# Two products for the centring, gate products ahead of LayerNorm's sums, and first weights held behind the squares, in a one-core RWKV-7 and Conformer step

## The chip, the core and the metric

The kernel runs on one core of a Trainium2 chip. A core has five engines that run side by side, each through its own list of instructions in a fixed order: TensorE (PE) multiplies matrices, VectorE (DVE) does elementwise work of one or two operands, ScalarE (ACT) does elementwise functions, GpSimd (POOL) and SyncE (SP) hardly compute here and SP issues DMAs. An engine goes on until an instruction needs something that another engine has not finished; then it and all that stands behind it in its list waits. The metric is the device time of one execution in microseconds (us), the median of several.

## The reference, cut to what matters

One layer takes 2048 new tokens of one sequence ("prompt") and one token for each of 8 running sequences ("samples"). The lines below are the core of the reference; the parts that the change touches are the norms `mu`/`var` over 64 channels of a head, the norm `cm`/`cv` over 512 channels, and the state `conv_new`.

```
h = rms_norm(x, norm_pre_g)
proj = h @ w_in                       # r, k, v, z_r, two LoRAs, conv GLU, z_c, two gates
...                                   # token shift, decay, in-context rate
y_w, wkv_new = wkv7_scan(...)         # delta rule, per head, 16 heads of 64
mu = mean(y_w, axis=-1); var = mean((y_w - mu)**2, axis=-1)      # per head
y_gn = (y_w - mu) * rsqrt(var + GN_EPS) * gn_g + gn_b
branch_r = ((y_gn + bonus) * silu(z_r)) @ w_branch_r
u = u_in[..., :D_CONV] * sigmoid(u_in[..., D_CONV:])
c = depthwise_conv(concat([conv_st, u]), conv_w) + conv_b        # 31 taps
cn = (c - cm) * rsqrt(cv + LN_EPS) * ln_c_g + ln_c_b             # over 512 channels
branch_c = (silu(cn) * silu(z_c)) @ w_branch_c
conv_new = buf[:, -(CONV_W - 1):]
out = (sigmoid(g_r) * branch_r + sigmoid(g_c) * branch_c) @ w_out
y = x + rms_norm(out, norm_post_g)
```

## The kernel before

**Tiling.** The prompt's 2048 tokens go through in four blocks of 512 (`BS`). Channels lie on the 128 partitions, tokens along the free axis, so a usual tile is 128 x 512 f32. Block 0 also carries 8 columns of the samples, so its input products are 128 x 264 (two halves of 256 + 8). In each block eight "units" (pairs of heads, `unit_a` and `unit_b`, j = 0 to 7) run the delta rule.

**Products.** Large matrix products are f32 products made of three passes over the high and the low parts of both operands. A value is split by `split` (L136): the high part is an ACT copy to a narrower type (fp32r), the low part is a DVE subtraction of the high part from the value. A product of two operands kept as full f32 is done by the PE in two records for each 512 columns instead of one. Weights come from DRAM to `wraw` over SP's queue, are split into `w` (`load_split`, L144) and stored once more ("kept") for later blocks.

**Centring of the group norm.** After a unit's recurrence its outputs lie in the one PSUM bank named `py`. ACT copies the bank to the tile `gt`, the PE multiplies `gt` by the matrix `cent` (the identity less 1/64 within each head) as one full f32 product into the next `py` (helper `stat`, L366), ACT squares that, `ones_b` sums it into `pc`, and the scaling follows. There are 32 units, so 32 such products. Tiles of one tag share a fixed number of buffers: `tmp` 4, `x` 2, `gt` 1, `xs` 1, `wraw` 3, `w` 5; PSUM banks: `pg` 3, `pa` 2, `pb`, `pc` and `py` one each.

**The order.** The code is written block by block, and a list scheduler orders each engine's instructions ahead of the run by priority; `behind(...)` and `issue_after` make an instruction come after a given one in that order. The tables `FILL0`, `FILL1`, `FILL2` say which pieces of other work (conv products `u`, gates by number, "n" for LayerNorm's mean, "z" and "Z" for the two halves of the z gate) are written behind which unit of a block, so that the PE has products to do while a unit's chain of small steps is running. `FILL0` belongs to block 0.

**LayerNorm of the conv branch.** `conv_norm` (L764) adds four tiles on DVE, averages over channels with a product by `avg_c`, and subtracts; `conv_scale` (L775) squares, averages again, and applies scale and sigmoid. `conv_gate` (L794) does the product of the z gate, its sigmoid, and the last multiplication; each z gate tile lies in `tmp`.

**The start.** `stage_first` (L391) loads x by eight transfers, squares the eight tiles on ACT, adds on DVE, averages by a product with `avg_c` (`py<-tmp,avg_c`), takes Ln and Exp on ACT, scales x and splits it into `ht`. `gemm_first` (L433) loads and splits the first weights and does the first 192 products.

**Samples.** Their work ("decode") is put between the prompt's work of blocks 1 and 2. Small copies (128 x 8) take the samples' columns out of PSUM in block 0 on DVE. One DRAM to DRAM copy moves the samples' conv state.

Of the kernel before, what the change touches and what calls it, by code (L numbers as in the profile page):

```python
# [25 lines left out]
def rwkv7_conformer_step(  # L26
# [8 lines left out]
    BS = 512  # L35
# [164 lines left out]
    cent = const.tile([128, 128], F32, name="cent")  # L200
# [3 lines left out]
    stt(cent, ones_b, -1.0 / 64, ident, ALU.mult, ALU.add)  # L204
# [96 lines left out]
    FILL0 = ("u1", "u2", "u3", "u5", "6n", "7", "0", "4zZ")  # L301
# [46 lines left out]
    def shift_(b, v, q, dst):  # L348
        mu = pv("mu", q)
        for ps, sl in v.parts:  # L350
            act(dst[:, sl], ps, AF.Identity, scale=omm[:, q:q + 1])
        before = None if b == 0 else carry[:, q:q + 1]
        for ps, sl in v.parts:
            n = sl.stop - sl.start
            d = dst[:, sl]
            stt(d[:, 1:n], ps[:, 0:n - 1], mu, d[:, 1:n], ALU.mult, ALU.add)
            if before is not None:
                stt(d[:, 0:1], before, mu, d[:, 0:1], ALU.mult, ALU.add)
            before = ps[:, n - 1:n]
# [30 lines left out]

    def stage_first():  # L391
# [41 lines left out]
    def gemm_first(ht, cols):  # L433
# [3 lines left out]
        for h in range(2):  # L437
            for c0 in cols:
                ws[c0, h] = new([128, 2, 4, 128], "w", F32R)
                load_split(ws[c0, h], win(c0)[h], ("in", c0 // 128, h))  # L440
# [219 lines left out]
    def unit_b(b, j, parts):  # L660
# [49 lines left out]

        ys = new([128, BS], "gt")
        cp(ys, yps)
        pcen = stat(pyt, cent, ys)
# [31 lines left out]
    def glu(b, ht, ct):  # L745
# [3 lines left out]
        with tc.high_priority(HPU):  # L749
# [14 lines left out]
    def conv_norm(b, cs):  # L764
# [5 lines left out]
        with tc.issue_after(done[0].ins):  # L770
# [4 lines left out]
    def conv_scale(b, cs):  # L775
# [7 lines left out]
        with tc.issue_after(done[0].ins):  # L783
# [3 lines left out]
        for ct in range(CT):  # L787
# [4 lines left out]
            mul(cs[ct], cs[ct], s1)  # L792

    def conv_gate(b, ht, cs, c0):  # L794
        vs = gemm([hspec(b, ht, N_SHIFT + 2 * DC + (c0 + i) * 128) for i in range(2)])
        s2s = []
        for i, z in enumerate(vs):
            ct = c0 + i
            s2 = new([128, BS], "tmp")
            s2s.append(s2)  # L800
            with tc.high_priority(HPZ):
                sigmoid_v(s2, z)
                for ps, sl in z.parts:
                    mul(s2[:, sl], s2[:, sl], ps)
                if b == 0:
                    vcp(sconv[:, 2 * CT + ct, :], z.s[0])
# [145 lines left out]
    def decode_conv():  # L952
# [13 lines left out]
        with later(5000):  # L966
            nc.scalar.dma_start(out=nconv_s[0, :, 0:NH - 1, :], in_=state_conv[0, :, 1:NH, :])
# [11 lines left out]
        vcp(un[0:NS], ps[0:NS])  # L979
# [34 lines left out]
    def gate(b, ht, i0):  # L1014
# [3 lines left out]
        with tc.high_priority(HPG):  # L1018
            for i, v in enumerate(vs):
                for ps, sl in v.parts:  # L1020
                    act(s[:, i, sl], ps, AF.Exp, scale=-1.0)
                if b == 0:
                    vcp(gate_s[:, i0 + i, :], v.s[0])
# [42 lines left out]
    def stage_out(b, mg):  # L1066
# [15 lines left out]
        def finish(i):  # L1082
# [14 lines left out]
            nc.scalar.dma_start(out=yout, in_=osb[i][0:n])  # L1097

        for h in range(2):
# [53 lines left out]
    def fill(b, ht, cs, what):  # L1153
# [3 lines left out]
        elif what == "n":  # L1157
            while taps:
                pull(1)
            conv_norm(b, cs)  # L1160
# [133 lines left out]
```

## Time and profile before

| | |
|---|---|
| median of 3 runs | 2791.29 us (2786.7 to 2793.33) |
| profiled execution, its own time | 2793.45 us |
| its span | 2791.7 us |
| PE busy | 2675.3 us (96%) |
| PE weight loads (PEld) busy | 2133.7 us (76%) |
| DVE busy | 1768.0 us (63%) |
| ACT busy | 1388.4 us (50%) |
| DMA, mean | 164 GB/s |

The span is the stretch from the first to the last event of the trace; the execution's own time holds 1.8 us more around it. Busy time is time in which an engine has an instruction in work; a wait is idle time that ended when another engine, or a DMA, signalled. A product of the PE overlaps the next one, so that the time of one product in a row of them is the distance of their starts, not the duration that stands beside one.

### The profile page before, as it was taken

How to read it: one execution, taken by the hardware profiler on the slowest of the kernel's cores; microseconds unless marked ns; L12 is line 12 of the kernel's file. 1: busy time of each engine (PE TensorE's matmuls, PEld its weight loads, DVE VectorE, ACT ScalarE, POOL GpSimd, SP SyncE). 2: the span in 40 equal slices, each digit the busy share in tenths (PEclk: the TensorE clock that was granted, in tenths of full speed). 3: DMA queues.
4: the chain of work that ended last, by engine and by line, in shares of the span. 5: the costliest groups of instructions: out<-in, count | busy, mean ns of one | idle time of the engine just before them, and what ended most of it. 6: DMA issues, size and time to landing. Idle time of an engine off the chain costs nothing.

```text
span 2791.7 us, 55435 instructions
## 1 busy us (share of the span) xinstructions
PE 2675.3 (96%) x22800; PEld 2133.7 (76%) x22800; DVE 1768.0 (63%) x3856; ACT 1388.4 (50%) x3039; POOL 16.2 (1%) x61
## 2 busy tenths in 40 slices
PE   6999999989999998999999999999999999999998
PEld 6888888878877776776887777677798777777787
DVE  5688887667876547556576646676376755664412
ACT  5666656672344555656113565755411356566511
POOL 0000000000000000000000000000000000000000
PEclk9999999999999899999999999999999999999999
DMA  6555654547974253344666324244466522332484
GB/s 215 184 166 179 196 179 167 188 136 257 312 248 135 86 146 114 109 147 130 212 235 214 129 94 156 100 134 150 154 215 215 193 95 100 96 114 92 132 280 166
DMA packets 149648, 458.50 MB, mean 164 GB/s; under 512 B 18897, under 2 KB 24258, under 8 KB 149387
## 3 DMA queue, kind: packets, MB, share of 16 engines
q1 hardware_dynamic: 143441, 433.36, 47.0%
q10 hardware_dynamic: 5954, 21.60, 1.9%
q8 instruction: 179, 2.93, 0.4%
q14 instruction: 74, 0.61, 0.1%
HBM read 346.21 MB, written 109.16 MB: 163 GB/s over the span
## 4 chain that ended last, share of the span: by engine, by line
PE 58%; DVE 20%; ACT 14%; DMA 4%; issue 2%; SPq 0%; POOL 0%; DVEq 0%; ACTq 0%; POOLq 0%
PE pg L112 41%; PE pa L112 7%; DVE gd L100 4%; PE pc L112 4%; PE py L112 4%; DVE zr L610 4%; PE pb L112 2%; ACT sc L94 2%; DVE et L106 2%; DVE raw L106 2%; DMA wraw<-in_w_in_dram 2%; ACT tmp L94 2%; ACT xv L94 2%; ACT zbuf L94 1%; ACT keep L94 1%
## 5 line engine op out<-in xcount | busy, mean ns | idle before, releaser
L112 PE MATMUL pg<-ht,w 128*128 128x512 f32 (+1 forms) x7200 | 1539.8, 365 | 18.2 <-DVE sconv L109 6.5
L112 PEld LDWEIGHTS pg<-ht,w 128*128 128x128 f32 x7200 | 1172.8, 190 | 264.6 <-issue 63.9
L106 DVE SCALAR_TENSOR_TENSOR et<-u,cw,et 128x512 f32<-128x512 f32 x480 | 359.5, 749 | 8.2
L94 ACT ACTIVATE raw<-pg,omm 128x512 f32<-128x512 f32 (+1 forms) x155 | 93.8, 605 | 194.0 <-PE pg L112 189.8
L94 ACT ACTIVATE tmp<-tmp 128x512 f32<-128x512 f32 (+1 forms) x305 | 185.5, 630 | 5.0 <-DVE tmp L106 2.5
L112 PE MATMUL pg<-orr,w 128*128 128x512 f32 (+2 forms) x960 | 184.7, 349 | 0.0
L112 PEld LDWEIGHTS pg<-orr,w 128*128 128x128 f32 x960 | 154.7, 188 | 25.0 <-DVE x L100 0.2
L94 ACT ACTIVATE w<-wraw 128x512 fp32r<-128x512 f32 x162 | 101.4, 629 | 119.5 <-PE pg L112 70.5
L106 DVE SCALAR_TENSOR_TENSOR raw<-pg,prm,raw 128x511 f32<-128x511 f32 (+1 forms) x185 | 103.8, 573 | 84.6 <-ACT raw L94 83.8
L100 DVE TENSOR_TENSOR gd<-zr,gp 128x144 f32<-128x144 f32 (+10 forms) x512 | 139.9, 273 | 15.2
L610 DVE TENSOR_REDUCE zr<-gd 128x16 f32<-128x32 f32 (+15 forms) x512 | 136.9, 267 | 13.9 <-DVE gd L100 0.2
L100 DVE TENSOR_TENSOR w<-wraw,w 128x512 fp32r<-128x512 f32 x162 | 110.6, 685 | 46.3 <-ACT w L94 45.2
L94 ACT ACTIVATE gd<-sc 32x128 f32<-32x128 f32 x256 | 78.6, 307 | 114.5 <-DVE sc L100 108.4
L528 DVE TENSOR_TENSOR_SCAN tmp<-scanm,tmp 128x512 f32<-128x512 bf16 x32 | 39.1, 1223 | 137.3 <-ACT tmp L94 137.3
L94 ACT ACTIVATE xs<-pc,dk 128x64 f32<-128x64 f32 x224 | 70.2, 313 | 106.5 <-PE pc L112 106.0
L100 DVE TENSOR_TENSOR x<-x,pg 128x512 f32<-128x512 f32 (+1 forms) x80 | 46.1, 578 | 101.5 <-PE pg L112 36.4
L112 PE MATMUL pa<-ar,bk 64*64 64x128 f32 x2048 | 101.3, 279 | 5.2 <-DVE bk L100 3.1
L112 PEld LDWEIGHTS pa<-ar,bk 64*64 64x64 f32 x2048 | 77.5, 132 | 37.1 <-DVE bk L100 15.1
L94 ACT ACTIVATE x<-pg 128x512 f32<-128x512 f32 (+1 forms) x80 | 40.9, 511 | 123.7 <-PE pg L112 119.9
L100 DVE TENSOR_TENSOR sc<-pa,maskw 128x512 f32<-128x512 f32 x128 | 82.5, 684 | 30.7 <-PE pa L112 30.3
L94 ACT ACTIVATE sc<-pa 64x256 f32<-64x256 f32 (+1 forms) x192 | 73.1, 381 | 47.0 <-PE pb L112 43.7
L100 DVE TENSOR_TENSOR keep<-pa,raw 128x512 f32<-128x512 f32 x32 | 22.1, 692 | 109.5 <-PE pa L112 109.5
(359 smaller groups left out, 3694.8 us busy)
## 6 DMA issues: line engine op xcount, KB each, us to landing
w<-kept_in SPq DMA_DIRECT2D x366, 512.0 KB, 3.4
kept_in<-w SPq DMA_DIRECT2D x122, 512.0 KB, 3.8
wraw<-in_w_in_dram SPq DMA_DIRECT2D x122, 256.0 KB, 3.2
w<-kept_br SPq DMA_DIRECT2D x48, 512.0 KB, 4.1
w<-kept_out SPq DMA_DIRECT2D x40, 512.0 KB, 4.5
gate<-x ACTq DMA_DIRECT2D x24, 512.0 KB, 4.7
x<-gate SPq DMA_DIRECT2D x48, 256.0 KB, 4.1
w<-kept_bc SPq DMA_DIRECT2D x24, 512.0 KB, 3.2
```

The lines of the kernel that those rows point to most:

```text
L94: return nc.scalar.activation(out=out, in_=in_, func=func, scale=scale, bias=bias, **kw)
L100: return nc.vector.tensor_tensor(out=out, in0=a, in1=b, op=op)
L106: return nc.vector.scalar_tensor_tensor(out=out, in0=a, scalar=s, in1=b, op0=op0, op1=op1)
L112: return nc.tensor.matmul(out=out, lhsT=lhsT, rhs=rhs, start=start, stop=stop, **kw)
L528: nc.vector.tensor_tensor_scan(out=sw, data0=scanm.rearrange("p c t -> p (c t)"), data1=sw, initial=0.0, op0=ALU.mult, op1=ALU.add)
L610: nc.vector.tensor_reduce(out=zl[:, 0:n, t:t + 2], in_=pr[:, 0:n, :, 0:w], axis=AX.X, op=ALU.add)
```

## The change

1. The centring. `cent` is kept as fp32r. The unit's outputs are split: high part by an ACT copy into `gt`, low part by a DVE subtraction into tag `xs`. Two products, `cent` by high and `cent` by low, go into the next `py` bank in place of one f32 product.
2. LayerNorm. In block 0 the table puts "z" behind unit 5, "Z" and gate 7 behind unit 6, gates 0 and 4 behind unit 7. The mean (`conv_norm`) is written behind the first half's z product, the scale (`conv_scale`) behind the second half's; the z tiles move from `tmp` to tag `x`, and the multiplication by them into `conv_scale`.
3. The start. The splits of the first weights come behind the last square (ACT) and the last addition (DVE).
4. The samples' small copies of block 0 go from DVE to ACT (94 of them).
5. The DRAM to DRAM copy of the conv state goes from the start to a place behind a copy of the decode work in block 1.
6. The last block's end: its square goes to a scratch tile, the multiplication by `gb` is done on DVE ahead of the scale, and one DVE instruction and one DMA stand for each half.

```
-    cent = const.tile([128, 128], F32, name="cent")
+    cent_r = const.tile([128, 128], F32R, name="cent")
...
-    FILL0 = ("u1", "u2", "u3", "u5", "6n", "7", "0", "4zZ")
+    FILL0 = ("u1", "u2", "u3", "u5", "6n", "z", "Z7", "04")
...
-                vcp(sraw[:, i, q, :], v.s[i])
+                cp(sraw[:, i, q, :], v.s[i])
...
-                tt(rb, rb, sq, ALU.add)
+                added = tt(rb, rb, sq, ALU.add)
+        first[:] = last.ins, added.ins
...
+        with behind(*first):
+            for h in range(2):
+                for c0 in cols:
+                    ws[c0, h] = new([128, 2, 4, 128], "w", F32R)
+                    load_split(ws[c0, h], win(c0)[h], ("in", c0 // 128, h))
...
+        yh = new([128, BS], "gt", F32R)
+        yl = new([128, BS], "xs", F32R)
+        split(yh, yl, yps)
+        pcen = pyt()
+        mm(pcen, cent_r, yh, stop=False)
+        mm(pcen, cent_r, yl, start=False)
         ys = new([128, BS], "gt")
-        cp(ys, yps)
-        pcen = stat(pyt, cent, ys)
         act(ys, pcen, AF.Square)
...
-                vcp(sconv[:, ct, :], va.s[0])
-                vcp(sconv[:, CT + ct, :], vb.s[0])
+                cp(sconv[:, ct, :], va.s[0])
+                cp(sconv[:, CT + ct, :], vb.s[0])
...
+            mul(cs[ct], cs[ct], zgate[ct // 2][:, ct % 2])
...
-        s2s = []
+        s2 = zgate[c0 // 2] = new([128, 2, BS], "x")
...
-        if c0 == 0:
-            conv_scale(b, cs)
-        for i, s2 in enumerate(s2s):
-            mul(cs[c0 + i], cs[c0 + i], s2)
+        (conv_scale if c0 else conv_norm)(cs)
...
-        with later(5000):
-            nc.scalar.dma_start(out=nconv_s[0, :, 0:NH - 1, :], in_=state_conv[0, :, 1:NH, :])
...
-        vcp(un[0:NS], ps[0:NS])
+        with behind(cp(un[0:NS], ps[0:NS]).ins):
+            nc.scalar.dma_start(out=nconv_s[0, :, 0:NH - 1, :], in_=state_conv[0, :, 1:NH, :])
...
-                    stt(osb[i][0:n, hs], pts[i][0:n] if h else osb[i][0:n, hs], rstd[0:n], gb[0:n, hs],
-                        ALU.mult, ALU.mult)
-                    tt(osb[i][0:n, hs], osb[i][0:n, hs], xrs[i][0:n, hs], ALU.add)
+                    stt(osb[i][0:n, hs], osb[i][0:n, hs], rstd[0:n], xrs[i][0:n, hs], ALU.mult, ALU.add)
+                    (nc.scalar, nc.sync)[h].dma_start(out=yout[:, hs], in_=osb[i][0:n, hs])
...
-                    act(half, pts[i][0:n], AF.Square, accum_out=sq[i][0:n, h:h + 1])
-                    if not (b == NB - 1 and h == 1):
+                    if b == NB - 1:
+                        junk = new([128, 512], "tmp")
+                        act(junk[0:n], pts[i][0:n], AF.Square, accum_out=sq[i][0:n, h:h + 1])
+                        mul(half, pts[i][0:n], gb[0:n, h * 512:h * 512 + 512])
```

Three places in the engines' order. First DVE at the start, before: `w_329` and `w_336` are the first two weights of the first product (the subtraction makes their low parts), `tmp_219` the sum of squares, `x_200` and `x_201` the first four tiles of x.

```order
L100 TENSOR_TENSOR w_329<-wraw_330,w_329 128x512
L100 TENSOR_TENSOR tmp_219<-tmp_219,tmp_233 128x512
L100 TENSOR_TENSOR tmp_219<-tmp_219,tmp_236 128x512
L100 TENSOR_TENSOR tmp_219<-tmp_219,tmp_239 128x512
L100 TENSOR_TENSOR w_336<-wraw_337,w_336 128x512
L100 TENSOR_TENSOR w_343<-wraw_344,w_343 128x512
```

And DVE at the start now, from the last addition's neighbour to the first weight's low part (the scalings and splits of x in between are cut).

```order
L100 TENSOR_TENSOR tmp_219<-tmp_219,tmp_239 128x512
L226 TENSOR_REDUCE par_c_119<-ident_79 128x2
L109 COPY cw_129<-pb_130 128x124
L106 SCALAR_TENSOR_TENSOR x_200<-x_200,prm_127,tmp_219 128x512
...
L106 SCALAR_TENSOR_TENSOR orr_203<-orr_203,prm_127,tmp_219 128x512
L100 TENSOR_TENSOR ht_280<-pa_252,ht_280 128x2x8
L100 TENSOR_TENSOR w_329<-wraw_330,w_329 128x512
L100 TENSOR_TENSOR ht_280<-orr_203,ht_280 128x256
```

The low part of `w_329` stood between two additions, ahead of every scaling of x; now it is the last but one of the list that scales and splits all eight tiles of x. On the PE, twelve products stand ahead of the first that reads it.

Second, the PE around the centring of a unit of block 1, before: `py` and `pc` are the banks of the unit, `pg<-ht,w` are products of the next gate or projection.

```order
L112 MATMUL py_11969<-aw_11903,xs_11926 64x64 x2
L112 MATMUL pg_12365<-ht_8009,w_12363 128x512
L112 MATMUL pg_12365<-ht_8010,w_12363 128x512 x3
L112 MATMUL py_12004<-gt_12002,cent_100 128x512
L112 MATMUL pg_12365<-ht_8011,w_12363 128x512 x3
```

And the same place now.

```order
L112 MATMUL py_12001<-aw_11935,xs_11958 64x64 x2
L112 MATMUL pg_12401<-ht_8040,w_12399 128x512 x2
L112 MATMUL pg_12401<-ht_8041,w_12399 128x512 x3
L112 MATMUL pg_12401<-ht_8042,w_12399 128x512 x3
L112 MATMUL py_12038<-gt_12034,cent_100 128x512
L112 MATMUL py_12038<-xs_12035,cent_100 128x512
L112 MATMUL pg_12440<-ht_8035,w_12436 128x512 x3
```

Between the unit's last output product and the centring stood four large products; now eight do, and the centring is two records of one product each.

Third, the PE at the samples' LoRA products in block 1 (`pb<-u,orr`, eight columns each, sixteen in all), before.

```order
L112 MATMUL pg_11170<-ht_8009,w_11168 128x512 x2
L112 MATMUL pb_10591<-u_10582,orr_10588 128x8
L112 MATMUL pg_11170<-ht_8009,w_11168 128x512
L112 MATMUL pb_10591<-u_10582,orr_10588 128x8
L112 MATMUL pg_11170<-ht_8010,w_11168 128x512
L112 MATMUL pb_10591<-u_10582,orr_10588 128x8
L112 MATMUL pg_11170<-ht_8010,w_11168 128x512
```

And now.

```order
L112 MATMUL pg_11237<-ht_8036,w_11233 128x512
L112 MATMUL pb_10625<-u_10616,orr_10622 128x8 x8
L112 MATMUL pg_11237<-ht_8036,w_11233 128x512
L112 MATMUL pg_11237<-ht_8037,w_11233 128x512 x3
L112 MATMUL pb_10634<-u_10616,orr_10622 128x8 x8
```

The small products alternated one by one with large ones; now they stand in two groups of eight.

## Rows read from the trace of the kernel before

**Rows 1.** The page's first part: engine, busy us, share of span, instructions.
```profile
PE   2675.3 (96%) x22800; PEld 2133.7 (76%) x22800; DVE 1768.0 (63%) x3856; ACT 1388.4 (50%) x3039; POOL 16.2 (1%) x61
```

**Rows 2.** Waits of PE by releaser: us in total, times, longest us.
```profile
PE pb L112 <- DVE gd L612: 20.2, 22, 2.2
PE py L112 <- DVE tmp L100: 15.0, 1, 15.0
PE pg L112 <- DVE tmp L100: 10.9, 2, 6.8
...
PE pg L112 <- DVE sconv L109: 6.5, 4, 1.9
```

**Rows 3.** Timeline of the start: start, us, engine, line, operation, [idle before].
```profile
11.26 1.32 ACT L94 ACTIVATE tmp<-orr 128x512 f32<-128x512 f32 x2
15.92 0.63 ACT L94 ACTIVATE w<-wraw 128x512 fp32r<-128x512 f32 x1 [3.35 <-DMA wraw<-in_w_in_dram]
...
17.20 2.28 DVE L100 TENSOR_TENSOR tmp<-tmp 128x512 f32<-128x512 f32 x3
...
19.62 2.05 PE L112 MATMUL py<-tmp,avg_c 128*128 128x512 f32 x2 [14.98 <-DVE tmp L100]
...
21.70 0.69 ACT L94 ACTIVATE tmp<-py,eps_rms 128x512 f32<-128x512 f32 x1 [0.16 <-PE py L112]
...
24.24 0.63 ACT L94 ACTIVATE tmp<-tmp 128x512 f32<-128x512 f32 x1 [0.23 <-DVE ht L100]
...
24.90 2.74 DVE L106 SCALAR_TENSOR_TENSOR x<-x,prm,tmp 128x512 f32<-128x512 f32 x4 [0.68 <-ACT tmp L94]
...
26.37 1.03 PE L112 MATMUL pg<-ht,w 128*128 128x264 f32 x3 [2.58 <-ACT ht L94]
```

**Rows 4.** Timeline of PE where the first 192 products end.
```profile
52.12 0.53 PE L112 MATMUL py<-ht,w 128*128 128x264 f32 x3
52.48 1.75 PE L112 MATMUL pg<-ht,w 128*128 128x264 f32 x13
```

**Rows 5.** Timeline of a unit's centring in block 1.
```profile
997.63 1.65 PE L112 MATMUL pg<-ht,w 128*128 128x512 f32 x6
...
997.99 0.61 ACT L94 ACTIVATE gt<-py 128x512 f32<-128x512 f32 x1
...
999.11 1.02 PE L112 MATMUL py<-gt,cent 128*128 128x512 f32 x2
...
1001.13 1.02 PE L112 MATMUL pc<-gt,ones_b 128*128 128x512 f32 x2
...
1001.99 1.02 PE L112 MATMUL pa<-tmp,ones_b 128*128 128x512 f32 x2
```

**Rows 6.** Timeline of PE, a run of large products in the last block.
```profile
2689.78 4.54 PE L112 MATMUL pg<-orr,w 128*128 128x512 f32 x19
2694.15 0.39 PE L112 MATMUL pg<-xv,w 128*128 128x512 f32 x1
```

**Rows 7.** Groups by form: DVE's low parts (count: ns min/median/max, first and last start).
```profile
L100 DVE TENSOR_TENSOR orr<-gt,orr x32: 675/684/694, 133.5 to 2642.1; 128x512 fp32r<-128x512 f32 x32
```

**Rows 8.** Timeline at a small copy in block 0.
```profile
152.57 0.16 DVE L109 COPY sconv<-pg 128x8 f32<-128x8 f32 x1
...
152.78 1.57 PE L112 MATMUL pg<-ht,w 128*128 128x264 f32 x10 [1.94 <-DVE sconv L109]
```

**Rows 9.** Windows: length, busy us of PE, PEld, DVE, ACT, POOL; PEclk; DMA.
```profile
612.00:628.00 16.00, 11.98 (x47) 9.67 (x48) 14.14 (x26) 11.36 (x21) 0.00 (x0) 0.79 0.29 83
...
1100.00:1112.00 12.00, 6.78 (x18) 4.78 (x19) 12.00 (x32) 5.88 (x10) 0.00 (x0) 0.72 0.19 79
948.00:970.00 22.00, 22.00 (x62) 14.50 (x62) 7.88 (x29) 2.87 (x11) 0.00 (x0) 0.61 0.17 55
```

**Rows 10.** Groups by form within 948 to 970 us: count, busy us, mean ns.
```profile
L112 PE MATMUL pb<-u,orr 64*128 64x8 f32 x32 | 8.2, 329 | 0.0
```

**Rows 11.** Timeline of the last DVE work before the last DMA.
```profile
2786.70 1.28 DVE L100 TENSOR_TENSOR orr<-orr,x 128x512 f32<-128x512 f32 x2
```

More of the change, by code (lines that the diff above doesn't have):

```diff
@@ L203, in rwkv7_conformer_step @@
         nc.gpsimd.memset(ones_b[s, s], 1.0)
-    stt(cent, ones_b, -1.0 / 64, ident, ALU.mult, ALU.add)
+    stt(cent_r, ones_b, -1.0 / 64, ident, ALU.mult, ALU.add)
+    cent = f32(cent_r)
     id2 = const.tile([128, C], F32, name="id2")
@@ L389, in stage_a @@
         return ht
+    first = []
     def stage_first():
@@ L436, in gemm_first @@
         views, ws = [], {}
[L437 to L440, printed above, removed]
+        with behind(*first):
[3 more added lines that the diff above has]
+                    load_split(ws[c0, h], win(c0)[h], ("in", c0 // 128, h))
         for i, _ in enumerate(cols):
@@ L762, in glu, with conv_norm @@
         return acc
-    def conv_norm(b, cs):
+    def conv_norm(cs):
         sm = new([128, BS], "tmp")
@@ L769, in conv_norm @@
             tt(sm, sm, cs[ct], ALU.add)
-        with tc.issue_after(done[0].ins):
+        with behind(done[0].ins):
             ps = stat(pgt, avg_c, sm)
@@ L773, in conv_norm, with conv_scale @@
             tt(cs[ct], cs[ct], ps, ALU.subtract)
-    def conv_scale(b, cs):
+    def conv_scale(cs):
         sm = new([128, BS], "tmp")
@@ L782, in conv_scale @@
             tt(sm, sm, sq, ALU.add)
-        with tc.issue_after(done[0].ins):
+        with behind(done[0].ins):
             ps = stat(pgt, avg_c, sm)
@@ L792, in conv_scale @@
             mul(cs[ct], cs[ct], s1)
+            mul(cs[ct], cs[ct], zgate[ct // 2][:, ct % 2])
+    zgate = [None, None]
     def conv_gate(b, ht, cs, c0):
         vs = gemm([hspec(b, ht, N_SHIFT + 2 * DC + (c0 + i) * 128) for i in range(2)])
-        s2s = []
+        s2 = zgate[c0 // 2] = new([128, 2, BS], "x")
         for i, z in enumerate(vs):
-            ct = c0 + i
-            s2 = new([128, BS], "tmp")
-            s2s.append(s2)
             with tc.high_priority(HPZ):
-                sigmoid_v(s2, z)
+                sigmoid_v(s2[:, i], z)
                 for ps, sl in z.parts:
-                    mul(s2[:, sl], s2[:, sl], ps)
+                    mul(s2[:, i, sl], s2[:, i, sl], ps)
                 if b == 0:
-                    vcp(sconv[:, 2 * CT + ct, :], z.s[0])
-        if c0 == 0:
-            conv_scale(b, cs)
-        for i, s2 in enumerate(s2s):
-            mul(cs[c0 + i], cs[c0 + i], s2)
+                    cp(sconv[:, 2 * CT + c0 + i, :], z.s[0])
+        (conv_scale if c0 else conv_norm)(cs)
     def conv_split(b, cs):
@@ L1022, in gate @@
                 if b == 0:
-                    vcp(gate_s[:, i0 + i, :], v.s[0])
+                    cp(gate_s[:, i0 + i, :], v.s[0])
         act(s, s, AF.Ln, bias=1.0)
@@ L1096, in finish @@
                 tt(osb[i][0:n], osb[i][0:n], xrs[i][0:n], ALU.add)
-            nc.scalar.dma_start(out=yout, in_=osb[i][0:n])
+                nc.scalar.dma_start(out=yout, in_=osb[i][0:n])
         for h in range(2):
@@ L1117, in sums @@
                     half = osb[i][0:n, h * 512:h * 512 + 512]
-                    act(half, pts[i][0:n], AF.Square, accum_out=sq[i][0:n, h:h + 1])
-                    if not (b == NB - 1 and h == 1):
+                    if b == NB - 1:
+                        junk = new([128, 512], "tmp")
+                        act(junk[0:n], pts[i][0:n], AF.Square, accum_out=sq[i][0:n, h:h + 1])
+                        mul(half, pts[i][0:n], gb[0:n, h * 512:h * 512 + 512])
+                    else:
+                        act(half, pts[i][0:n], AF.Square, accum_out=sq[i][0:n, h:h + 1])
                         cp(half, pts[i][0:n])
@@ L1159, in fill @@
                 pull(1)
-            conv_norm(b, cs)
         elif what in "zZ":
```

## The prediction

> **What bounds the kernel now.** I read the page's busy times first, then the waits of the PE, then the timeline at each of its longest waits, and the windows for the clock there. The PE is busy for 2675.3 us, 96% of a span of 2791.7 [rows 1]: it is the bound, and what it does not fill is 116 us. So the change can gain only where it takes PE work away, closes a wait of the PE, or lets the PE run at its full 2.4 GHz where it ran at 1.2; work moved between DVE (63%) and ACT (50%) counts only where the PE waits for it. The list of PE waits [rows 2] names the places: 15.0 us once at the start, 10.9 us in two waits for LayerNorm's sums (6.8 and so 4.1), 6.5 us in four waits for a small copy, and 20.2 us in 22 waits for small DVE steps of the units (`gd`), which no edit touches. The windows [rows 9] show the second cost: around the two LayerNorm waits the granted clock is 0.79 and 0.72, and around the samples' LoRA products, where the PE never idles, 0.61.
>
> All sums are made against the profiled execution's own 2793.45 us (its span and 1.8 us around it). The median shown is 2791.29, lower by 2.16, which I take off at the end.
>
> **The centring (32 units).** A full f32 product of 128 x 512 takes 1001.99 - 1001.13 = 0.86 us from start to start, in two records [rows 5]. A product of the new kind, with fp32r operands, is like those of the large run, 19 in 2694.15 - 2689.78 = 4.37 us, 0.23 each [rows 6]. One f32 product goes, two of the other kind come: 0.86 - 0.46 = 0.40 saved, 12.8 us over 32 units.
> Against it stands a new link in the chain. The centring waited for one ACT copy of 0.61 us; now for that copy and a DVE subtraction behind it, 0.68 us [rows 7]. The PE's order decides whether this shows. In the unit at 997 us six large products stand between the last output product and the centring, from 997.63 to 999.11, 1.48 us, and the PE did not wait [rows 5]. The copy begins 0.36 us into that stretch, so copy and subtraction need 0.36 + 0.61 + 0.68, with 0.1 between engines 1.75 us. In the new order seven or eight products stand there in most units, 1.6 to 1.85 us: cover about as long as the need, if DVE is free. It works 63% of the time [rows 1], so in some 20 of 32 units something can stand in its way for a part of 0.68; at a mean of 0.14 us that costs 2.8. I take -10. The bounds: -12.8 with nothing exposed, and +9 with the subtraction bare in every unit (32 x 0.68 = 21.8 less 12.8).
> The Trainium skill ("FP8 and Floating Point Precision", section "TensorE Precision Notes") says that a true FP32 product goes through the array in four passes. By it the product removed would cost 4 x 0.23 = 0.92 and the saving would be 14.7 us instead of 12.8; the trace shows two records that together take 0.86, and I keep the measured price.
>
> **The start.** Before, the squares on ACT stand still behind a weight's high part that waits for its transfer until 15.92 (3.35 us idle), so that the last additions run from 17.20 to 19.48; the sums' product starts at 19.62 after a wait of 14.98 us, its Ln at 21.70, the Exp at 24.24, and the scaling of x at 24.90 [rows 3]. Now the last two squares follow those at 11.26 directly, and the last addition ends at about 11.26 + 1.32 + 1.32 + 0.7 = 14.6. From there product 2.05, Ln 0.69, Exp 0.63 and three hand-overs: scaling starts at about 18.1, 6.8 us earlier. But the low part of the first weight, which DVE made between two additions, now stands behind nearly the whole scaling and splitting of x: eight scalings (4 in 2.74, so 5.5), seven low parts of 0.68 (4.8), the samples' scaling over twice the columns (1.4, an estimate from the low part's 0.68) and eight small ones (1.3, as the small copy of [rows 8]), 13.0 us, so that it comes at about 31. The PE has only twelve products that do not read it. Before, the first 192 products started at 26.37 and ended at 52.48 [rows 3, 4]. Now 180 remain at 31; at the 0.12 us of the stretch's end [rows 4] they take 22 us and end at 53, with the slower rate of the first products up to 55. So the 15 us wait does not go; it is replaced by one for the weight's low part. I take +1.4, bounds -1 (the eight transfers of x are done before 11.26, so the squares start earlier) to +4 (the kept copies, which hang on these low parts, delay the next weights on SP's queue).
> On that copy the Trainium skill ("DMA: Bandwidth & Descriptors", section "Issuing engines are not separate DMA queues") says that transfers issued by different engines run on the same 16 DMA engines. By that rule x would land earlier by a part of the copy's time; no run here shows it, and the term keeps its bound.
>
> **The small copies (block 0).** Four times a large product needs a bank that is free only after a DVE copy of 0.16 us, which stands behind a unit's chain of small steps (`zr`, `gd`) on DVE: 6.5 us in all, the longest 1.94 [rows 2, 8]. On ACT the copy follows directly the Exp that reads the same bank, and about 0.7 of the wait is left each time: 6.5 - 2.8 = 3.7 gained. A wait of 4.1 us goes with 3.4 us lost at the lower clock around it (below), so up to 0.8 us more for each one that goes, 3 here. I take -6. Bounds: -9 (waits and slow stretches all go) and -3 (half the waits, no clock). The other 82 copies move from DVE to ACT, which is idle half of the time; cost nothing here, and if ACT is late with them, 94 x 0.16 = 15 us are spread over block 0, most of it beside PE work.
>
> **LayerNorm's sums.** In block 0 the PE waited 4.1 us at the block's end and ran at 0.79 for 16 us (0.21 x 16 = 3.4 lost); with the mean behind the first z product and the scale behind the second, gates 0 and 4 come after it and cover the chain. But the z tiles now hold tag `x`, of which there are two, and gate 7's first tile needs one: it stands behind conv_scale's twenty ACT steps (about 0.63 each, 12.6 us), against some 11 us of products. That is a new wait of 1 to 5 us; with 2 for it the net is 4.1 + 3.4 - 2, or -5.5. In block 1 the wait is 6.8 us, at a clock of 0.72 over 12 us (0.28 x 12 = 3.4 lost) [rows 2, 9]: DVE was in use all 12 of 12 us by decode. Now the mean's sums stand ahead of that decode work in DVE's order. I leave 1 us of the wait and two thirds of the loss's return: -8. Bounds for both: -17, and 0 if the sums only queue elsewhere.
>
> **Decode's LoRA in block 1.** No line of the diff speaks of it, but the order moves it: sixteen small products of two records, which alternated with large ones, come in two groups of eight. In the window of 22 us the PE is busy throughout, at a mean of 0.61, so most of it at 1.2 GHz [rows 9]; the 32 records last 0.33 us each [rows 10], for eight columns. At 2.4 GHz throughout, the same work would take 0.61 x 22 = 13.4 us. With two short groups in place of one long mixed stretch I expect most of these 8.6 us back: -7. Bounds -8.6 (the clock never falls) and 0 (it falls as before).
>
> **The end.** The two last additions on DVE, 1.28 us [rows 11], leave the path to the last DMA: -1.2, bounds -1.4 and 0.
>
> **New waits.** All lists of DVE and ACT are shuffled, so some PE waits of 0.5 to 2 us will stand where none stood; the idle time not named above is 116 - 53 = 63 us. A twelfth of it again, +5 (0 to +12), stands for them.
>
> **The sum.** -10 + 1.4 - 6 - 5.5 - 8 - 7 - 1.2 + 5 = -31.3. 2793.45 - 31.3 = 2762.1 for the profiled execution; less 2.16, 2760.0 as a median.
>
> **The rivals.**
> *The subtraction stands bare (slower).* Copy and subtraction together are 1.29 us; if DVE reaches the subtraction late, the PE waits in each unit. The other edits bring -21.3, so the sum is slower by 0.2% (5.6 us) only when the centring costs +27, a wait of (27 + 12.8)/32 = 1.24 us in every unit: both steps bare. At 1.29 us the kernel lands at 2791.3 - 21.3 + 28.5 = 2798. For it: one `py` bank, so nothing can start before the subtraction has read it. Against it: seven or eight products between. Half of it, the subtraction alone bare, gives 2791.3 - 21.3 + 9 = 2779.
> *Waits only move.* DVE in use throughout the 12 us around LayerNorm in block 1 speaks for it: with the sums earlier, decode's own steps come later, and the PE meets these; LoRA's pace stays. Then LayerNorm's 13.5 and the LoRA's 7 do not come: 2760 + 20.5 = 2780. Against it: the PE had products that need nothing from decode.
> *The start and gate 7 cost more.* Start +4, gate 7's wait 5 with the slow clock behind it: 7 to 10 more, 2769.
> *More clock comes back.* The three windows alone lose 3.4 + 3.4 + 8.6 = 15.4 us to the clock [rows 9]. With centring, copies and LoRA at their better bounds (2.8, 3 and 1.6 more) and no new waits (5): 2760 - 12.4 = 2748. Against it: gate 7, which shows a new wait in the order itself.
>
> **How the numbers follow.** Forecast 2760, 0.50, own range 2750 to 2770; waits only move 0.16; subtraction bare by half 0.10, in full 0.05; start and gate 7 0.11; more clock 0.08. The range from 2742 to 2783 takes in all but the full rival and the far parts of the halves. A change under 0.2%, about 5.6 us, cannot be told from none here. Faster than that (below 2785.7): all of forecast, more clock, and start, most of the two at 2780, 0.86 together; same 0.08; slower 0.06.
>
> **What would show it.** Right: `py<-gt,cent` and `py<-xs,cent` follow at 0.23 us and the PE's waits for DVE `xs` add up to under 4 us; waits for `sconv` under 3; no wait of over 2 us for `tmp` by `avg_c` in blocks 0 and 1; decode's LoRA done in 9 us; at the start a new PE wait for DVE `w`, with the first 192 products done at 53 to 55. Wrong: `xs` among the first waits with 20 us or more; the low part of the first weight on time; gate 7's products waiting over 5 us for `tmp` or `x`; a clock of 0.6 still around the LoRA.

## The result and the profile after

The changed kernel takes 2766.86 us (median of 5, 2762.79 to 2768.61); the kernel before, run beside it, 2793.33 (median of 5, 2786.70 to 2795.25). The ratio is 0.9909, 95% interval 0.9894 to 0.9923: 26.5 us less, where 31.3 were forecast and 2760 was the time named. The execution that was profiled after is the fastest of its five (2762.79), 4 us under the median, so the two traces differ by 30.7 us; what follows reads traces against each other, and medians where a time is judged.

The page after, first part: busy us, share of the span of 2761.1 us, instructions.

```profile
PE 2655.0 (96%) x22800; PEld 2126.7 (77%) x22800; DVE 1781.1 (65%) x3793; ACT 1390.3 (50%) x3130; POOL 16.1 (1%) x61
```

Against [rows 1] the PE is busy 20.3 us less, and the span is 30.6 less, so that its idle time fell from 116.4 to 106.1. The PE is as full as before; two thirds of the gain are work that it no longer does or does at the higher clock (the mean granted clock of the trace is 0.993 where it was 0.990), one third is waits. DVE has 13 us more to do: the 32 subtractions are 22, the copies that left it are under 15, and the other 6 are not accounted for here.

The PE's waits after, to be read against [rows 2] (us in total, times, longest).

```profile
PE pb L112 <- DVE gd L617: 17.4, 23, 1.3
PE py L112 <- DVE tmp L100: 9.5, 1, 9.5
...
PE pa L112 <- DVE bk L100: 6.8, 9, 2.0
PE pb L112 <- ACT gp L94: 6.4, 5, 3.2
...
PE pg L112 <- ACT sconv L94: 4.4, 7, 0.9
...
PE pa L112 <- DVE ht L100: 3.7, 1, 3.7
...
PE pa L426 <- DVE orr L106: 3.4, 1, 3.4
```

No wait for `xs`, the centring's new operand, is among them. The 10.9 us for LayerNorm's sums are gone. New are 3.7 and 3.4 us at the start; `bk` rose from 3.1 to 6.8 and `gp` from 3.9 to 6.4. These two before:

```profile
PE pb L112 <- ACT gp L94: 3.9, 3, 2.0
...
PE pa L112 <- DVE bk L100: 3.1, 8, 0.6
```

The centring of the unit that [rows 5] showed (timeline: start, us).

```profile
1002.01 2.12 PE L112 MATMUL pg<-ht,w 128*128 128x512 f32 x8
...
1002.22 0.59 ACT L94 ACTIVATE gt<-py 128x512 fp32r<-128x512 f32 x1
...
1002.84 0.69 DVE L100 TENSOR_TENSOR xs<-py,gt 128x512 fp32r<-128x512 f32 x1
...
1003.96 0.39 PE L112 MATMUL py<-gt,cent 128*128 128x512 f32 x1
...
1004.19 0.39 PE L112 MATMUL py<-xs,cent 128*128 128x512 f32 x1
...
1004.42 1.56 PE L112 MATMUL pg<-ht,w 128*128 128x512 f32 x6
```

Two products in 1004.42 - 1003.96 = 0.46 us, where the f32 product took 0.86. Eight large products stand over copy and subtraction: from 1002.01 to 1003.96 is 1.95 us, and the subtraction ends at 1003.53, 0.4 us in time. In none of the 32 units does the PE idle before the pair.

The start (timeline), against [rows 3, 4].

```profile
13.64 2.05 PE L112 MATMUL py<-tmp,avg_c 128*128 128x512 f32 x2 [9.52 <-DVE tmp L100]
...
21.28 1.33 PE L112 MATMUL pg<-ht,w 128*128 128x264 f32 x4 [0.27 <-ACT ht L94]
...
28.62 0.69 DVE L100 TENSOR_TENSOR w<-wraw,w 128x512 fp32r<-128x512 f32 x1
...
28.85 0.78 PE L112 MATMUL pa<-ht,w 128*128 128x264 f32 x2 [3.73 <-DVE ht L100]
...
53.80 1.38 PE L112 MATMUL pg<-ht,w 128*128 128x264 f32 x10
```

Sums 6.0 us earlier, first product 5.1 us earlier, and the first 192 products are done 1.3 us later (53.80 against 52.48). Two things hold the PE until 28.85, one directly after the other. The product that waits needs the second `pa` bank, which the samples' columns occupy until DVE has made the last of their small low parts (the profile names it: DVE `ht`). The `pg` products behind it need the first weight's low part, which DVE begins only at 28.62 and ends at 29.31; they start at 29.43, so that the PE would have waited anyway.

Four windows, as [rows 9] (length, busy us of PE, PEld, DVE, ACT, POOL; PEclk; DMA).

```profile
612.00:628.00 16.00, 16.00 (x98) 13.65 (x97) 9.41 (x15) 11.03 (x23) 0.00 (x0) 1.00 0.50 165
...
1100.00:1112.00 12.00, 12.00 (x53) 9.71 (x52) 11.55 (x34) 1.38 (x2) 0.00 (x0) 1.00 0.62 187
1140.00:1162.00 22.00, 17.32 (x171) 12.79 (x170) 16.56 (x27) 14.59 (x30) 0.00 (x0) 0.84 0.25 82
...
948.00:970.00 22.00, 21.72 (x156) 16.30 (x156) 12.57 (x31) 11.59 (x33) 0.00 (x0) 0.77 0.18 58
```

The two places of LayerNorm have a full PE and a granted clock of 1.00 (2.4 GHz). Part of block 1's loss moved 45 us on (experiment 3): between 1140 and 1162 the PE now idles 4.7 us, mostly for `bk`, at a clock of 0.84, where it idled 0.6 us at a clock of 1.00. Around decode's LoRA the clock rose from 0.61 to 0.77.

Decode's LoRA itself, sixteen products in 32 records (timeline of the PE), with its first row before:

```profile
948.61 0.39 PE L112 MATMUL pb<-u,orr 64*128 64x8 f32 x2
```

And now:

```profile
946.54 1.95 PE L112 MATMUL pb<-u,orr 64*128 64x8 f32 x16
948.42 1.87 PE L112 MATMUL pg<-ht,w 128*128 128x512 f32 x4
950.22 3.58 PE L112 MATMUL pb<-u,orr 64*128 64x8 f32 x16
953.73 1.22 PE L112 MATMUL pg<-ht,w 128*128 128x512 f32 x2
```

From 946.54 to 953.73 are 7.2 us; before it was 16.9, from 948.61 to 965.48, where a run of eleven large products begins. But 16 large products stood in that stretch and four stand in this one; twelve at 0.23 [rows 6] are 2.8 us that are done elsewhere now, so that 6.9 us are gained. The first group runs at 0.12 us a record, the second at 0.22: the granted clock is 1.00 from 946.0 to 948.4 and 0.50 from 950.2 to 953.7.

The end, against [rows 11].

```profile
2756.74 1.41 DVE L106 SCALAR_TENSOR_TENSOR orr<-orr,rstd,x 128x512 f32<-128x512 f32 x2
...
2758.18 0.33 SPq L1098 DMA_DIRECT2D out_dram<-orr  x1
```

The last DMA is issued 2.9 us before the end of the span, where it was 3.7 (2788.02 of 2791.7), and the last DVE work ahead of it takes 1.4 us where it took 2.6.

### The profile page after: what moved, and what is told of

Its sections match the earlier page's. It is cut to its first block, busy times and chain, and to the rows that moved or that the text cites. A ratio compares the mean times of both kernels' runs of the same rounds, so it can differ in the third digit from the quotient of the medians.

```text
span 2761.1 us, 55539 instructions
## 1 busy us (share of the span) xinstructions
PE 2655.0 (96%) x22800; PEld 2126.7 (77%) x22800; DVE 1781.1 (65%) x3793; ACT 1390.3 (50%) x3130; POOL 16.1 (1%) x61
## 4 chain that ended last, share of the span: by engine, by line
PE 60%; DVE 20%; ACT 14%; issue 2%; DMA 2%; SPq 0%; POOL 0%; DVEq 0%; POOLq 0%; ACTq 0%
PE pg L112 42%; PE pa L112 8%; DVE gd L100 5%; PE pc L112 4%; DVE zr L615 4%; PE py L112 4%; ACT sc L94 2%; PE pb L112 2%; ACT tmp L94 2%; ACT xv L94 2%; ACT zbuf L94 2%; DVE raw L106 2%; DVE et L106 1%; ACT keep L94 1%; DVE gp L596 1%
## 5 line engine op out<-in xcount | busy, mean ns | idle before, releaser
L112 PE MATMUL pg<-ht,w 128*128 128x512 f32 (+1 forms) x7200 | 1515.1, 361 | 12.3 <-ACT sconv L94 4.4
L94 ACT ACTIVATE tmp<-tmp 128x512 f32<-128x512 f32 (+1 forms) x273 | 166.1, 630 | 3.6 <-DVE tmp L106 2.0
L94 ACT ACTIVATE x<-pg 128x512 f32<-128x512 f32 (+1 forms) x100 | 50.8, 509 | 141.8 <-PE pg L112 141.5
L100 DVE TENSOR_TENSOR x<-x,pg 128x512 f32<-128x512 f32 (+1 forms) x100 | 57.3, 577 | 95.1 <-PE pg L112 45.3
L94 ACT ACTIVATE x<-x 128x1024 f32<-128x1024 f32 (+1 forms) x96 | 87.7, 913 | 1.5
```

Of the source, the lines that this page charges most:

```text
L94: return nc.scalar.activation(out=out, in_=in_, func=func, scale=scale, bias=bias, **kw)
L100: return nc.vector.tensor_tensor(out=out, in0=a, in1=b, op=op)
L112: return nc.tensor.matmul(out=out, lhsT=lhsT, rhs=rhs, start=start, stop=stop, **kw)
```

## The experiments

Each was timed against the kernel before on its own chip. That kernel took 2792.80 us beside experiments 1 to 4, 2793.86 beside 5 to 8 and 2790.78 beside 9 and 10. Where a difference to the changed kernel or to another experiment is given, it is that of the medians; between these groups it can be off by up to 3 us, and where that matters the difference of the gains over the kernel before is given too.

**1. The old centring in the changed kernel.**

```
...
-        split(yh, yl, yps)
-        pcen = pyt()
-        mm(pcen, cent_r, yh, stop=False)
-        mm(pcen, cent_r, yl, start=False)
+        cp(ys, yps)
+        pcen = stat(pyt, cent, ys)
```

> The changed kernel with the old centring (one ACT copy, one f32 product in two records) and all else as changed. Theory: the product is priced by the PE alone and the subtraction is covered, so 32 x 0.40 = 12.8 us come back: 2766.9 + 12.8 = 2779.7, give or take 4 for the reshuffled order; the wait of the PE for the centring's operands is zero in both. Rival A (the subtraction costs part of what the product saves): 2766.9 + 5 to 8 = 2773. Rival B (a full f32 product costs four passes of 0.23): 2766.9 + 14.7 = 2781.6, which only the starts of the products in the trace can tell from the theory.

Measured: 2781.06 us (2780.02 to 2786.37), ratio 0.9964 (0.9950 to 0.9977): 14.2 more than the changed kernel. A full f32 product still takes 0.86 us in its trace, so the third price, 0.92, is not what this chip charges, though the time alone (2781.6 expected by it) could not have told; 12.8 us of the 14.2 are the product, the other 1.4 are within the scatter. Rival A falls. That the rest is so small is in part luck: between the two profiles the PE's busy time differs by 20.1 us and not 12.8, with a granted clock of 0.991 in place of 0.993, and its idle time by 2.3 us the other way.

**2. The first weights' splits not held back.**

```
-        with behind(*first):
-            for h in range(2):
+        for h in range(2):
...
```

> The changed kernel with the first weights' splits not held behind the squares. Theory: the long first wait of the PE is back (about 13 to 15 us in place of 9.5), but the low parts are early, so the waits of 3.4 and 3.7 us behind it are gone and the first 192 products end at 52.5 to 53, 1 us earlier than the 53.8 of the changed kernel: time 2766 (-2 to +1). Rival (the shorter first wait is a gain that only appears later): the first products end at 56 or later and the time is 2770 or more.

Measured: 2765.76 (2763.37 to 2769.55), 1.1 less; the time is the theory's, but not for its reason. The order at the start is the same with and without the edit: the first wait is 9.5 us, the waits of 3.4 and 3.7 are there, and the first 192 products end at 54.07. So this line of the diff does nothing at the start; something else moved the splits. Experiment 8 shows what.

**3. LayerNorm's old places.**

```
-    FILL0 = ("u1", "u2", "u3", "u5", "6n", "z", "Z7", "04")
+    FILL0 = ("u1", "u2", "u3", "u5", "6n", "7", "0", "4zZ")
...
-        (conv_scale if c0 else conv_norm)(cs)
+        if c0 == 0:
+            conv_scale(b, cs)
```

> The changed kernel with the table, the mean, the scale and the z gate's tiles as before. Theory: the waits for LayerNorm's sums by avg_c (4 us at the end of block 0, 6.8 us in block 1) and the half clock around them return, and the new waits for bk near 1148 us go: net +8 to +14, 2775 to 2781. Rival (the waits only moved to the unit that comes next): net +0 to +4, 2767 to 2771.

Measured: 2779.19 (2774.90 to 2782.33), 12.3 more, within the theory's 8 to 14. Two waits of its PE tell where (us in total, times, longest):

```profile
PE pb L112 <- DVE gd L617: 25.2, 22, 6.4
PE pg L112 <- DVE tmp L100: 10.2, 2, 6.8
```

The 10.2 us are the two waits of [rows 2]. The 6.4 us for `gd` were not foreseen: they stand at 1767 us, in block 2, where steps of the z gate and of LayerNorm's sums (`tmp`, 128 x 512) stand between the unit's small steps on DVE. The kernel before had 2.2 us there, its longest of that kind [rows 2], and the changed kernel has 0.7. So LayerNorm's new place clears a third place too. From 1120 to 1180 us the PE waits 0.4 us for `bk` here and 3.5 us in the changed kernel, so those waits do come with the move. The parts of the edit (table, mean, scale, tag of the z tiles) were not undone one by one.

**4. The small copies back on DVE.**

```
-                cp(sraw[:, i, q, :], v.s[i])
+                vcp(sraw[:, i, q, :], v.s[i])
...
-                cp(sconv[:, ct, :], va.s[0])
-                cp(sconv[:, CT + ct, :], vb.s[0])
+                vcp(sconv[:, ct, :], va.s[0])
+                vcp(sconv[:, CT + ct, :], vb.s[0])
...
```

> The changed kernel with the 94 small copies of block 0 on DVE. Theory: the four waits for the copy of 1 to 2 us return in place of seven of 0.4 to 0.9 (6.5 against 4.4 us), the rest is noise of the order: +2 (0 to +6), 2769. Rival (the copies on ACT delay ACT's own chain in block 0 and cost as much as they bring, seen as more waits of PE for ACT in block 0 now): -3 to 0, 2765.

Measured: 2771.08 (2768.27 to 2772.44), 4.2 more. The waits for `sconv` are 8.8 us in place of 4.4, more than the 6.5 expected, and the longest new wait is another one (timeline of block 0):

```profile
306.95 0.63 ACT L94 ACTIVATE w<-wraw 128x512 fp32r<-128x512 f32 x1 [6.07 <-DMA wraw<-in_w_in_dram]
...
311.18 0.42 ACT L94 ACTIVATE lora_w<-wraw 128x256 fp32r<-128x256 f32 x1 [3.60 <-DMA wraw<-in_w_lora_dram]
311.50 0.46 ACT L94 ACTIVATE tmp<-pg,nglu 128x256 f32<-128x256 f32 x1
...
312.01 0.59 PE L112 MATMUL pg<-ht,w 128*128 128x264 f32 x1 [7.48 <-ACT tmp L94]
```

ACT stands still twice for a weight's transfer, and the Exp that would free the PE's bank stands behind. At the same place of the changed kernel ACT stands before a weight too, and the PE behind ACT, but less long (the profile names the PE for ACT's 5.18 us, though the PE's last product had ended 0.8 us before, so that a transfer may have been what it waited for; the rows do not settle it):

```profile
306.11 0.63 ACT L94 ACTIVATE w<-wraw 128x512 fp32r<-128x512 f32 x1 [5.18 <-PE pg L112]
...
308.56 1.06 PE L112 MATMUL pb<-zbuf,gp 32*32 32x32 f32 x32 [3.23 <-ACT gp L94]
```

Each of the two, 4.4 us more for `sconv` and 4.3 us more at this place, would make up the 4.2 alone; other waits grew as well (`bk` from 6.8 to 11.5) and others shrank (`gp` from 6.4 to 0.2). So the copies' worth is their own waits and what the order puts behind a late transfer, in shares that this run does not tell.

**5. The centring alone, in the kernel before.** The edit is that of the change's first part.

> The kernel before with the new centring alone. Its order also puts the conv state's copy late and the sixteen LoRA products of decode in two groups of eight, and holds the first weights behind the squares, all without the other edits. Theory (the order, not the diff's own line, brings the LoRA's gain): -12.8 for the centring, -7 to -9 for the LoRA, +1 for the start: 2792.8 - 19 = 2774 (2770 to 2778), LoRA done in 7 to 9 us. Rival (the centring alone acts): 2780, LoRA still 15 us or more.

Measured: 2789.03 (2785.63 to 2792.67, 11 runs), ratio 0.9982 (0.9973 to 0.9991): 4.8 us. The order that the expectation describes is not this kernel's own: its trace has the conv state's copy at 1.45 us, a first wait of 14.8 us and the LoRA alternating for 16.1 us, all as before. Then the rival's 2780 stands to be judged, and it fails too: 12.8 us of PE work are gone, and the time moved by 4.8. Its PE waits show where part of the rest went:

```profile
PE pb L112 <- DVE gd L613: 22.7, 21, 6.4
...
PE pg L112 <- ACT tmp L94: 7.9, 2, 7.3
```

The 7.3 us are the wait of experiment 4 at 304 us, the 6.4 that of experiment 3 in block 2; the kernel before has neither at that length. Both come from the new order, and each is closed by another part of the change: the copies on ACT, and LayerNorm's new place. In all, the PE idles 121.5 us where it idled 116.4, which is 5.1 of the 8.0 us taken back. The other 2.9 are busy time: it fell by 9.9 us and not by 12.8, at a mean granted clock of 0.987 in place of 0.990 (0.987 or 0.988 in all eleven runs, 0.989 to 0.992 in the fifteen of the kernel before beside them). That is why undoing the centring costs 14.2 and doing it alone brings 4.8.

**6. The centring's link made longer.**

```
         split(yh, yl, yps)
+        tt(yl, yps, f32(yh), ALU.subtract)
```

> The changed kernel with the DVE subtraction of the centring made twice (0.68 us more in each of the 32 chains, same result). Theory: large products placed between cover the longer link too, PE waits for xs under 3 us in all: 2766.9 (-2 to +4). Rival (the cover of 1.6 to 1.85 us is used up): each unit waits 0.4 to 0.7 us, 13 to 22 us more, 2780 to 2789, with xs among the first waits of the PE.

Measured: 2766.69 (2765.42 to 2769.72), 0.2 less than the changed kernel. The 64 subtractions take the 0.69 us of before each, and the list of PE waits names no `xs` from DVE. The scheduler, which counts the link too, puts more products over it: in most units of blocks 1 to 3 eleven, 2.8 us, where the changed kernel has seven or eight, 1.9 to 2.1 us. The cover is not used up. This also closes the prediction's slower rival.

**7. The first weights' low parts early.**

```
-        with behind(*first):
+        with behind(*first), tc.high_priority(30):
```

> The changed kernel with the first weights' splits at a higher priority, so that their low parts stand on DVE after the third scaling of x and not behind the seventh. Theory: the wait of 3.7 us for the low part at the start goes and the first 192 products end 3 to 5 us earlier (49 to 51 in place of 53.8): 2763 (2760 to 2766). Rival (the products then wait for the scalings of x that were moved back): the first products end at 53 to 54 and the time stays at 2766.9.

Measured: 2759.98 (2758.44 to 2761.79), ratio 0.9877 (0.9864 to 0.9891): 6.9 less than the changed kernel, at the far end of the theory's range. The first products end earlier than the 49 to 51 expected, and the trace has the reason:

```profile
21.08 0.67 DVE L100 TENSOR_TENSOR w<-wraw,w 128x512 fp32r<-128x512 f32 x1
...
21.43 2.59 PE L112 MATMUL pg<-ht,w 128*128 128x264 f32 x10 [0.27 <-ACT ht L94]
...
46.36 3.81 PE L112 MATMUL pg<-ht,w 128*128 128x264 f32 x30
```

The low part comes 7.5 us earlier, the PE begins at the same time as in the changed kernel and no longer stops: while the `pa` bank is still held, it has the low part's products to do, and the first 192 products end at 46.36 in place of 53.80.

**8. The conv state's copy back at the start.**

```
+        with later(5000):
+            nc.scalar.dma_start(out=nconv_s[0, :, 0:NH - 1, :], in_=state_conv[0, :, 1:NH, :])
...
-        with behind(cp(un[0:NS], ps[0:NS]).ins):
-            nc.scalar.dma_start(out=nconv_s[0, :, 0:NH - 1, :], in_=state_conv[0, :, 1:NH, :])
+        vcp(un[0:NS], ps[0:NS])
```

> The changed kernel with the conv state's copy of 464 KB at the start again, and the small copy of decode back on DVE. In its order the sixteen LoRA products alternate with large ones as before, and the first weights' low parts stand ahead of the scaling of x. Theory: LoRA 15 to 17 us in place of 7.3, so +7 to +9; start: the transfers of x take longer to issue (5.9 us in place of 2.4 for the last four), the low parts are early, first 192 products end at 52 to 56: 2774 (2771 to 2778). Rival (the LoRA's slow pace came from the clock of its surroundings, not from alternating): LoRA 8 to 10 us, 2767.

Measured: 2765.32 (2760.92 to 2769.46), 1.5 less, not the 4 to 11 more of the theory. Both halves of it are in the trace, but the start's has the other sign. The LoRA alternates and takes 16.0 us, with 16 large products in it:

```profile
946.04 0.39 PE L112 MATMUL pb<-u,orr 64*128 64x8 f32 x2
946.36 0.49 PE L112 MATMUL pg<-ht,w 128*128 128x512 f32 x1
946.78 0.38 PE L112 MATMUL pb<-u,orr 64*128 64x8 f32 x2
...
962.06 5.06 PE L112 MATMUL pg<-ht,w 128*128 128x512 f32 x11
```

And the first 192 products end at 48.44, 5.4 us earlier than in the changed kernel, because the order puts the low parts ahead of the scaling of x, with the PE running through. The LoRA is 8.8 us longer than in the changed kernel, of which twelve more large products are 2.8; so +6 and -5.4 stand against the measured -1.5, and that is within the scatter of the medians. The last four transfers of x do go out more slowly, as SP's queue shows here and in the changed kernel (start, us):

```profile
3.12 5.20 SPq L400 DMA_DIRECT2D orr<-in_x_cols_dram  x4
```

```profile
3.13 2.44 SPq L400 DMA_DIRECT2D orr<-in_x_cols_dram  x4
```

but that costs the sums only 1 us. So it is the copy's place that sets the order at the start (experiment 2's line does not), and moving it had cost 5 us there and, by luck of the order, grouped the LoRA. The edit also puts the small copy that the DMA hung on back on DVE; whether this one step has a part in either was not tested.

**9. Experiment 8 with the LoRA's products grouped.**

```
-                mm(ps[:, j * NS:j * NS + NS], w2[rs, j * 128:j * 128 + 128], xl[rs])
+                with tc.high_priority(3000):
+                    mm(ps[:, j * NS:j * NS + NS], w2[rs, j * 128:j * 128 + 128], xl[rs])
```

> The kernel with the conv state's copy at the start (the run before of that kind: LoRA alternating, 16.1 us, 2765.3) with one edit more: the sixteen LoRA products get a high priority, so that they stand in two groups of eight, as in the changed kernel. Theory (alternating is what made them slow): LoRA in 7 to 9 us, time 2765.3 - 8 = 2757 (2754 to 2761). Rival (what the group saves comes back as waits or half clock right behind it): 2763 to 2767 with LoRA in 7 to 9 us; or LoRA still above 12 us.

Measured: 2757.00 (2755.52 to 2759.40), ratio 0.9878 (0.9861 to 0.9896): 8.3 less than experiment 8, the theory's time; but the kernel before was 3.1 us faster beside this run, and by the gains over it the difference is 5.2. The traces stand between: from the LoRA's first product to the `pb<-u,ones_b` behind it are 20.9 us in experiment 8 (946.04 to 966.92) and 10.7 here (946.35 to 957.03), with twelve large products fewer, 2.8 us; 7.4 us are gained. The sixteen products:

```profile
946.35 1.95 PE L112 MATMUL pb<-u,orr 64*128 64x8 f32 x16
948.23 0.96 PE L112 MATMUL pg<-ht,w 128*128 128x512 f32 x3
949.12 3.13 PE L112 MATMUL pb<-u,orr 64*128 64x8 f32 x16
952.18 5.00 PE L112 MATMUL pg<-ht,w 128*128 128x512 f32 x12
```

Alternating has two costs. At full clock a product of two records and its large neighbour take 946.78 - 946.04 = 0.74 us; apart, the first is (948.23 - 946.35)/8 = 0.24 and a large one 0.23 [rows 6], so 0.27 us is lost at each change. And the granted clock from 946 to 970 us, which holds the slow stretch of either run whole, is 0.64 in experiment 8 and 0.86 in this one, as their windows show (first 8, then 9):

```profile
946.00:970.00 24.00, 24.00 (x74) 17.00 (x74) 9.04 (x37) 4.03 (x15) 0.00 (x0) 0.64 0.19 67
```

```profile
946.00:970.00 24.00, 24.00 (x193) 18.83 (x191) 12.13 (x54) 12.69 (x37) 0.34 (x1) 0.86 0.32 111
```

0.22 of 24 us is 5.3, which leaves 2.1 of the 7.4 for the alternation. Counted from the other side, six of the fourteen stretches of small products in experiment 8 run at full clock, 0.27 lost at each, and eight at half, where a pair takes 1.24 us (951.92 less 950.68) and apart 0.44 + 0.44 (the second group of the changed kernel, 3.51/8, and the large products behind experiment 8's LoRA, 4.86/11), so 0.36 lost: 4.5 us, which leaves 2.9 for the clock. The two costs overlap, since pairs that run at half clock are in both, and which is the larger is not shown.

**10. Only twelve of the copies on ACT, on top of experiment 7.**

```
-                cp(sraw[:, i, q, :], v.s[i])
+                vcp(sraw[:, i, q, :], v.s[i])
...
-                    cp(gate_s[:, i0 + i, :], v.s[0])
+                    vcp(gate_s[:, i0 + i, :], v.s[0])
```

> The kernel with the first weights' low parts early (2760.0) with 82 of the 94 small copies back on DVE: only the twelve copies of the conv and z products stay on ACT. Theory: the gain of the copies (4.2 us) comes from those twelve, since only they free the bank that the next product waits for; time 2760 (-3 to +1). Rival (the gain comes from ACT doing the others, DVE being the fuller engine in block 0): 2763 to 2765.

Measured: 2769.32 (2764.79 to 2772.17), 9.3 more than experiment 7 (12.4 by the gains over the kernel before). The theory falls: with the low parts early the other 82 copies are worth that much, twice what all 94 are in the changed kernel. They are not free of waits either: the changed kernel's list has 0.9 us for `gate_s`, one of theirs. What the twelve are worth by themselves was not run. Two PE waits stand out:

```profile
PE pa L112 <- DVE bk L100: 11.6, 9, 5.5
...
PE pg L112 <- ACT tmp L94: 8.5, 3, 6.4
```

In experiment 7 they are 6.4 and 0.7. The first is DVE, late in block 0 with 82 more steps; the second is again the place of experiment 4. How much of the 9.3 is DVE's load and how much the accident of order was not separated.

## Why the prediction was right, point by point

- **What bounds the kernel.** Right: the span fell by what the PE no longer does, no longer waits for, or does at the higher clock; the added DVE work of 22 us is seen in no wait of its own.
- **The centring.** The price was right (0.40 a unit, 12.8 us), the -10 too cautious: exposed was nothing, and even a link 0.68 us longer exposes nothing. The cover was taken as 1.6 to 1.85 us against a need of 1.75; it is 1.95 in the unit shown. What the step did not see is that a reshuffled order takes back more than half when the centring is alone (experiment 5), in waits and at the lower clock. The sum carried the waits under new waits and had no term for the clock.
- **The start.** +1.4 was forecast and +1.3 is in the trace, in part by luck. The low part was expected at about 31 and was done at 29.31; the 182 products then left took 53.80 - 28.85 = 24.95 us, 0.14 each and not 0.12, and the two misses cancel. The low part is also only half the cause: the `pa` bank held by the samples' columns stands in front of it, and the step did not see that (the sign "a new PE wait for DVE `w`" came as one for `ht`). Wrong too was the edit that it was laid to: holding the splits behind the squares changes nothing there; the conv state's copy does. The Trainium skill ("DMA: Bandwidth & Descriptors", section "Issuing engines are not separate DMA queues") has transfers of all issuing engines share the same 16 engines. The traces agree in so far as with the copy issued by ACT at the start (experiment 8) the issue of SP's last four took 5.20 us in place of 2.44, and the sums' product started 1.1 us later; how the transfers shared the engines no row here shows.
- **The small copies.** Forecast -6, undone 4.2. The waits themselves gave 2.1 us against the kernel before and not 3.7: what is left of each is about the 0.7 that was taken (0.6), but seven are left and not four, and the sign "waits for `sconv` under 3" failed with 4.4. What the other half of the 4.2 is, experiment 4 does not tell.
- **LayerNorm.** Forecast -13.5, undone 12.3. Gate 7's wait for a tile of tag `x` did not come (0.7 us for `x` is all, and that is in block 1); 4.7 us of waits near 1150 us, mostly for `bk`, came in its place.
- **The LoRA.** Forecast -7, and 6.9 us are gained in the changed kernel's trace (5.2 to 8.3 where it alone is changed, in experiment 9). The size was right, the reason half: the forecast laid it all to the clock, and the clock of the window from 948 to 970 rose by 0.16 of 22 us, 3.5. The rest goes with the alternation itself, which the step did not have; how much of it is which, experiment 9 leaves open.
- **The end.** Forecast -1.2; from the PE's end to the span's end it was 7.8 and is 5.9 us, so 2.0. No run undoes this part alone.
- **New waits.** This is the term that was mis-sized: +5 was taken, and the sum is 4.8 us short of the median. In block 0 alone the PE idles 28.0 us from 60 to 590 us, summed over its gaps in the trace, where it idled 22.1, though the `sconv` waits shrank by 2, and the clock of that stretch is 0.98 where it was 0.99; with the waits near 1150 us in block 1, new idle time is over 10.

Left open: how much of the difference between forecast and median is the choice of execution (the profiled one is 30.7 us under its counterpart, the medians 26.5). The prices of the single parts do not add up to the whole, since each was taken in another order; and the two best edits, experiments 7 and 9, were not run together.

## What to carry to other kernels

Under a list scheduler an edit's price is its work plus the order it happens to get, and the second can be the larger: 12.8 us of saved PE work brought 4.8 alone and 14.2 in company, and a moved DMA brought 6 at one end and cost 5 at the other. So read the changed order engine by engine for three things: what stands ahead of the first consumer's operand, which in-order engine stands behind a late transfer, and whether small products alternate with large ones. The two best versions here, 2757.0 and 2760.0 us (ratios 0.9878 and 0.9877, so alike), came from reading the order and moving sixteen products or four splits, not from saving work.

## What was not expected of the hardware

Eight-column products that alternate with 512-column ones cost 0.27 us for each change over what both take in groups, at full clock. And the PE's granted clock fell while such products ran, alternating or grouped (0.64 and 0.86 over the same 24 us in experiments 8 and 9), with the PE never idle: a PE that is busy by the profile is not a PE that keeps its clock.
